# Norm work from GpSimd to VectorE, float32 products inside the norms, and a gate in three groups

## The chip, the cores and the metric

The kernel runs on one core of a Trainium2 chip. The metric is the device time of one execution in microseconds (us). A core has a matrix engine (TensorE, PE in the profile), a vector engine (VectorE, DVE), a scalar engine (ScalarE, ACT), a general one (GpSimd, POOL) and an engine that here only issues transfers (SyncE, SP). Each engine works through its own row of instructions in order and waits on the others by semaphores.

## The reference

Two blocks follow one another on 512 tokens of width 1024, with two layers each. A layer of the first block has four parts, each behind a residual and a LayerNorm; the second block has RMS norms, attention and a memory of 256 tokens.

```python
def first_block(x, p, ...):
    for i in range(DEPTH):                      # DEPTH = 2, ALPHA = sqrt(2)
        x = layer_norm(ALPHA * x + 0.5 * swiglu(x, ffn_w_in[i, 0], ffn_w_out[i, 0]), ...)
        mix = token_mix(x, mix_w_in[i], ...)
        x = layer_norm(ALPHA * x + mix, ...)
        x = layer_norm(ALPHA * x + 0.5 * swiglu(x, ffn_w_in[i, 1], ffn_w_out[i, 1]), ...)
        ple = jax.nn.sigmoid(x @ ple_w_gate[i] + ple_b_gate[i]) * (p[i] @ ple_w_proj[i])
        x = layer_norm(ALPHA * x + ple, ...)
    return x

def second_block(x, mem, ...):
    for i in range(DEPTH):                      # layer A: dilated attention, layer B: axial
        h = rmsnorm(x, norm_g[i])
        mem_h = rmsnorm(mem, mem_norm_g[i])
        ...
        o_mem = memory_attention(q_mem, mem_h, w_mem_kv[i], ...)   # kv = mem_h @ w_kv
        y = jnp.concatenate([o_mix, o_mem], axis=-1) * jax.nn.silu(gate)
        x = x + jnp.einsum('bse,ed->bsd', y, w_out[i])
    return x
```

The embedding p[i] is 512 x 256, ple_w_proj[i] is 256 x 1024, ple_w_gate[i] 1024 x 1024, w_mem_kv[i] 1024 x 1024.

## The kernel before

Features lie on the 128 partitions: x is eight feature tiles (KD = 8) of 128 x 512 tokens. Most work on tokens goes in two halves of 256 (HALF), so that one half's norm can run under the other half's products.

**Split products.** A float32 product is made of three products in a reduced type (fp32r in the profile): both operands are split into a high part (a cast on ScalarE) and a low part (x minus the high part), and hi·hi, hi·lo and lo·hi are summed in PSUM. `weight` (L146) loads a weight, casts `whi` (L153) and subtracts `wlo` (L154), on VectorE or on GpSimd as the caller says; `mm3` (L190) and `mm3k` (L1151) issue the products.

**A LayerNorm** (class LN, L258) is fed by `add`, tile by tile: x is updated and its sum `ln_s` and square sum `ln_q` grow along the features (L296, L299 to L303). For the first tile a mean is estimated and subtracted from all eight (L283, L285). `begin` sums over the partitions by TensorE (`ln_st`, L315), makes mean and reciprocal root from them by some 17 tiny operations on 128x2 (L319 to L323 and `rsqrt` at L231 to L239), spreads both over the partitions by TensorE (`ln_M`, `ln_B`, L253) and subtracts the mean (L332). `end` multiplies by the root (L343), applies scale and bias on ScalarE (L345), and writes the split result `xh`, `xl` (L352, L353) for the next products.

**A layer of the first block** runs ffn(l, 0), mixer, ffn(l, 1) and ple (L1015), each with the norm of its end inside. An FFN's weights come as units; its last output tile is made half by half, and the first half's `begin` lies between the halves. `ple` first splits p and its projection matrix and makes the embedding (`ppp`, 96 fp32r products), then the gate (`pg`): feature tiles 0 to 3 at once, in four PSUM tiles (`mm3_side`), for both halves, then 4 to 7 for each half; a sigmoid (`sig`, L1055) and a product with the embedding end each tile and free its PSUM.

**Memory.** In layer 1's ple the memory tokens are normalized and split (`mem_parts`), and layer A's keys and values (`p_mkv`) are made in three pieces between the steps of the gate and its norms; the RMS norm of layer A follows (`from_time`, `scale_time`, `write_time`). Layer B's keys and values are made between layers A and B (L1773).

**Order.** The tile framework's scheduler orders each engine's row, the transfers on SP's queue too; in the mixer TensorE's order is woven by hand. What is ready when depends on the buffer pools: five slots each for high and low parts of weights, two for loaded weights, and four each for two kinds of PSUM tiles.

Of the kernel before, what the change touches and what calls it, by code (L numbers as in the profile page):

```python
# [33 lines left out]
class Kern:  # L34
# [124 lines left out]
    def unit(self, src, eng=None, spare=False):  # L159

        if not spare:
            hi, lo = self.weight(src, D, eng)
            return [tuple(a[:, k * 128:k * 128 + 128] for a in (hi, lo)) for k in range(KD)]
        nc = self.nc
        st = self.pst.tile([128, D], F, name="wst", tag="wst")
        nc.sync.dma_start(out=st, in_=src)
        out = []
        for at in (slice(0, 512), slice(512, 1024)):
            hi, lo = self.t2(dt=FR, name="gwh"), self.t2(dt=FR, name="gwl")
            nc.scalar.copy(hi, st[:, at])  # L170
            (eng or nc.vector).tensor_sub(lo, st[:, at], hi.bitcast(F))
            out += [tuple(a[:, k * 128:k * 128 + 128] for a in (hi, lo)) for k in range(4)]
        return out
# [841 lines left out]
def ple(K, l, x, xh, xl, ln, rms=None, aside=None):  # L1015

    nc = K.nc
    V, A, G = nc.vector, nc.scalar, nc.gpsimd
# [3 lines left out]
    ph, pl = [], []  # L1022
    for k in range(2):
        st = K.t2(name="p_st")
        nc.sync.dma_start(out=st, in_=K.i["p"][l, :, k])
        ph.append(K.t2(dt=FR, name="p_h"))
        pl.append(K.t2(dt=FR, name="p_l"))
        K.split(ph[k], pl[k], st)
    Wp = []
    for j in range(2):  # L1030
        a, b = K.weight(K.i["ple_w_proj"][l, :, j * D:j * D + D], D)
        Wp.append((a.rearrange("p (f k c) -> p f k c", f=4, k=2), b.rearrange("p (f k c) -> p f k c", f=4, k=2)))

    pp = []
    for f in range(KD):
        p = K.acc(name="ppp")
        K.mm3(p, [((Wp[f // 4][0][:, f % 4, k], Wp[f // 4][1][:, f % 4, k]), (ph[k], pl[k])) for k in range(2)])
        c = K.t2(name="pp")
        A.copy(c, p)
        pp.append(c)  # L1040

    def unit(f, spare=False):
        return K.unit(K.i["ple_w_gate"][l, f], None if spare else nc.gpsimd, spare)

    def some(fs, W, tk):

        ps = {f: K.acc((128, 256), name="pg") for f in fs}
        parts = [(xh[:, k, tk], xl[:, k, tk]) for k in range(KD)]
        if fs[0] == 0:
            K.mm3_side([(ps[f], W[f], parts) for f in fs])  # L1050
# [871 lines left out]
```

## Time and profile before

| | us |
|---|---|
| median of 3 runs (lowest to highest) | 3540.33 (3538.97 to 3543.59) |
| the profiled execution, its own time | 3544.78 |
| its span in the trace | 3543.0 |
| TensorE busy | 3410.4 |
| VectorE busy | 1946.4 |
| ScalarE busy | 1245.0 |
| GpSimd busy | 723.7 |

Busy is the time in which an instruction of the engine was under way in the trace; the span is the time from the profile's first event to its last, and 1.8 us of the execution lie outside of it. The profile is of one execution, and its time is 4.5 us above the median of the runs.

### The profile page before, as it was taken

What the parts mean: (1) busy time and instruction counts of PE and PEld (TensorE: products, weight loads), DVE (VectorE), ACT (ScalarE), POOL (GpSimd) and SP (SyncE); (2) the same over time, 40 slices, a digit from 0 to 9 for tenths busy, and PEclk for the clock granted to TensorE, in tenths of its full rate; (3) what the DMA queues carried; (4) which work ended last, traced back from release to release, by engine and by line L of the source; (5) the groups of instructions that cost most, each with busy time, mean ns of one, the idle gap of its engine ahead of it and who ended that gap; (6) DMA issues with size and microseconds to landing.
All of it is one profiled execution on the core that took longest, in us unless ns stands there. A gap on an engine that the chain in (4) does not pass through costs nothing. (4 is left out here: it accounts for less than half of the span.)

```text
span 3543.0 us, 46065 instructions
## 1 busy us (share of the span) xinstructions
PE 3410.4 (96%) x17964; PEld 2900.1 (82%) x17964; DVE 1946.4 (55%) x4167; ACT 1245.0 (35%) x2104; POOL 723.7 (20%) x560
## 2 busy tenths in 40 slices
PE   8999999999999799999999999987999999999998
PEld 7888987788887788888978888876888888887777
DVE  3333665563334733346665533367867767649665
ACT  3322435332223332224353322244333333334332
POOL 0002412450012500123135200234122212111100
PEclk9999999999999899999999999997999999999999
DMA  4323211123232132232011222333222222243112
GB/s 154 109 87 98 85 36 49 37 84 101 95 92 87 48 107 98 87 93 84 34 36 61 84 100 87 98 97 122 86 85 71 69 87 73 75 133 115 54 47 79
DMA packets 91657, 294.40 MB, mean 83 GB/s; under 512 B 14256, under 2 KB 16944, under 8 KB 91312
## 3 DMA queue, kind: packets, MB, share of 16 engines
q1 hardware_dynamic: 91440, 291.47, 25.4%
q8 instruction: 141, 2.31, 0.3%
q14 instruction: 76, 0.62, 0.1%
HBM read 283.96 MB, written 7.47 MB: 82 GB/s over the span
## 5 line engine op out<-in xcount | busy, mean ns | idle before, releaser
L154 DVE TENSOR_TENSOR wlo<-wst,whi 128x1024 fp32r<-128x1024 f32 (+1 forms) x403 | 479.4, 1190 | 726.5 <-ACT whi L153 722.5
L153 ACT CAST whi<-wst 128x1024 fp32r<-128x1024 f32 (+1 forms) x520 | 530.3, 1022 | 881.1 <-issue 305.3
L188 PE MATMUL pgu<-xh,wlo 128*128 128x512 f32 (+1 forms) x1504 | 569.0, 379 | 0.2 <-ACT silu L374 0.2
L188 PE MATMUL pgu<-xl,whi 128*128 128x512 f32 (+1 forms) x1504 | 564.7, 378 | 0.0
L154 POOL TENSOR_TENSOR wlo<-wst,whi 128x1024 fp32r<-128x1024 f32 x117 | 282.0, 2416 | 577.0 <-ACT whi L153 566.7
L188 PE MATMUL pgu<-xh,whi 128*128 128x512 f32 (+1 forms) x1504 | 385.4, 379 | 12.3 <-ACT xh L176 9.1
L188 PEld LDWEIGHTS pgu<-xh,whi 128*128 128x128 f32 x1504 | 287.3, 191 | 63.8 <-ACT xh L176 9.1
L188 PEld LDWEIGHTS pgu<-xh,wlo 128*128 128x128 f32 x1504 | 287.6, 191 | 51.8 <-ACT silu L374 0.6
L188 PEld LDWEIGHTS pgu<-xl,whi 128*128 128x128 f32 x1504 | 285.0, 191 | 51.9 <-DVE xl L177 0.8
L1157 PE MATMUL p_in<-whi,xl 128*128 128x512 f32 (+1 forms) x800 | 305.1, 383 | 5.8 <-DVE xl L1307 4.5
L1157 PE MATMUL p_in<-wlo,xh 128*128 128x512 f32 (+1 forms) x800 | 305.8, 383 | 0.0
L1157 PE MATMUL p_in<-whi,xh 128*128 128x512 f32 (+1 forms) x800 | 305.2, 382 | 0.0
L285 POOL TENSOR_TENSOR x<-x,ln_c 128x256 f32<-128x256 f32 (+1 forms) x84 | 95.9, 1174 | 970.5 <-ACT ln_c L282 970.5
L188 PE MATMUL pfo<-hl,whi 128*128 128x512 f32 (+1 forms) x792 | 282.7, 366 | 0.0
L188 PE MATMUL pfo<-hh,wlo 128*128 128x512 f32 (+1 forms) x792 | 282.3, 365 | 0.0
L375 DVE TENSOR_TENSOR silu<-silu,pgu 128x512 f32<-128x512 f32 (+1 forms) x94 | 61.4, 653 | 225.1 <-PE pgu L188 190.9
L188 PE MATMUL pmx<-xl,whi 128*128 128x512 f32 (+1 forms) x480 | 180.3, 379 | 0.0
L1157 PEld LDWEIGHTS p_in<-whi,xl 128*128 128x128 f32 x800 | 151.6, 189 | 33.9 <-DVE xl L1307 4.6
L188 PE MATMUL pmx<-xh,wlo 128*128 128x512 f32 (+1 forms) x480 | 178.7, 373 | 0.0
L1157 PEld LDWEIGHTS p_in<-wlo,xh 128*128 128x128 f32 x800 | 151.7, 190 | 27.7 <-issue 2.6
L1157 PEld LDWEIGHTS p_in<-whi,xh 128*128 128x128 f32 x800 | 151.5, 189 | 27.6 <-issue 2.4
L188 PEld LDWEIGHTS pfo<-hh,wlo 128*128 128x128 f32 x792 | 149.4, 189 | 24.2
(376 smaller groups left out, 6468.7 us busy)
## 6 DMA issues: line engine op xcount, KB each, us to landing
wst<-in_ffn_w_in SPq DMA_DIRECT2D x176, 512.0 KB, 3.4
wst<-in_ffn_w_out SPq DMA_DIRECT2D x64, 512.0 KB, 3.5
wst<-in_wa_qk SPq DMA_DIRECT2D x48, 512.0 KB, 3.3
wst<-in_ffn_w_out SPq DMA_DIRECT2D x32, 384.0 KB, 3.1
wst<-in_mix_w_qkv SPq DMA_DIRECT2D x24, 512.0 KB, 3.5
wst<-in_wa_v SPq DMA_DIRECT2D x24, 512.0 KB, 3.3
wst<-in_w_gate SPq DMA_DIRECT2D x24, 512.0 KB, 3.2
wst<-in_w_out SPq DMA_DIRECT2D x32, 384.0 KB, 3.1
```

The costliest lines, as they stand in the source:

```text
L153: nc.scalar.copy(hi, st)
L154: sub = (eng or nc.vector).tensor_sub(lo, st, hi.bitcast(F))
L188: return self.nc.tensor.matmul(out, lhsT=lhsT, rhs=rhs, start=start, stop=stop)
L285: nc.gpsimd.tensor_sub(self.y[:, k, tk], self.y[:, k, tk], c)
L375: nc.vector.tensor_mul(s, s, ps[1])
L1157: K.nc.tensor.matmul(out, lhsT=w, rhs=x, start=(j == 0), stop=(j == n - 1))
```

## The change

Four things are done together.

1. GpSimd's work in the norms and the weight splits goes to VectorE: the mean's subtractions (84), the square sums (60), the low parts `xl` (56, for which the cast `xh` goes from VectorE to ScalarE), and 116 of the 117 `wlo` of 128x1024, of which 16 vanish with the splits below.
2. The embedding is a class of its own, `Embed`. It loads p and the projection unsplit (three transfers of 512 KB, into slots of the split weights) and multiplies in plain float32, one call in place of three products. Its 16 calls for feature tiles 0 to 3 are issued after the FFN's last output tile, the other 16 after the second half's `begin`.
3. The gate has three groups: feature tiles 0 to 3 side by side for each half, tile 4 for both halves in one PSUM tile, and 5 to 7 for each half.
4. The memory's keys and values are plain float32 products too, for both layers, in layer 1's norms; the results wait in DRAM. Nothing of it is left between layers A and B.

```diff
+    def raw(self, pool, src, n):
+        t = pool.tile([128, n], F, name="wraw", tag="whi" if pool is self.pwh else "wlo")
+        self.nc.sync.dma_start(out=t, in_=src)
+        return t
...
-                nc.gpsimd.tensor_sub(self.y[:, k, tk], self.y[:, k, tk], c)
+                nc.vector.tensor_sub(self.y[:, k, tk], self.y[:, k, tk], c)
...
-        if f < KD - 2:
-            nc.gpsimd.tensor_add(q, q, sq)
-        elif f == KD - 2:
+        if f == KD - 2:
...
-                nc.vector.tensor_copy(xh[:, ks, tk], y)
-                nc.gpsimd.tensor_sub(xl[:, ks, tk], y, xh[:, ks, tk].bitcast(F))
-def ffn(K, l, j, x, xh, xl, ln, aside=None, load=None):
+                nc.scalar.copy(xh[:, ks, tk], y)
+                nc.vector.tensor_sub(xl[:, ks, tk], y, xh[:, ks, tk].bitcast(F))
...
-        wh, wl = K.weight(w_in[l, j, 2 * f + u], D, nc.gpsimd if (f < 4 if load is None else f == 0 and u) else None)
+        wh, wl = K.weight(w_in[l, j, 2 * f + u], D, nc.gpsimd if load and f == 0 and u else None)
...
     W = out_units(KD - 1)
+    if ahead:
+        ahead.load()
     out_tile(KD - 1, W, HALF[0])
     ln.begin(HALF[0])
     out_tile(KD - 1, W, HALF[1])
+    if ahead:
+        ahead.products(0, 4)
     ln.end(HALF[0], xh, xl)
     ln.begin(HALF[1])
+    if ahead:
+        ahead.products(4, KD)
     ln.end(HALF[1], xh, xl)
...
-        wh, wl = K.weight(src, D, nc.gpsimd)
+        wh, wl = K.weight(src, D)
...
+class Embed:
+    def __init__(self, K, l):
+        self.K, self.l, self.out = K, l, []
+    def load(self):
+        K, i = self.K, self.K.i
+        self.p = K.raw(K.pwh, i["p"][self.l].rearrange("p k s -> p (k s)"), D).rearrange("p (k s) -> p k s", k=2)
+        self.W = [K.raw(K.pwl, i["ple_w_proj"][self.l, :, j * D:j * D + D], D).rearrange("p (f k c) -> p f k c", f=4, k=2)
+                  for j in range(2)]
+    def products(self, f0, f1):
+        K = self.K
+        for f in range(f0, f1):
+            p = K.acc(name="ppp")
+            for k in range(2):
+                K.mm(p, lhsT=self.W[f // 4][:, f % 4, k], rhs=self.p[:, k], start=(k == 0), stop=(k == 1))
+            c = K.t2(name="pp")
+            K.nc.scalar.copy(c, p)
+            self.out.append(c)
...
+    def some(f, W, tk):
+        p = K.acc((128, tk.stop - tk.start), name="pg")
+        K.mm3(p, list(zip(W, [(xh[:, k, tk], xl[:, k, tk]) for k in range(KD)])))
+        add(f, p, tk)
...
+    first, last = range(4), range(5, KD)
+    W = [K.unit(K.i["ple_w_gate"][l, f]) for f in first]
+    for tk in HALF:
+        ps = [K.acc((128, 256), name="pg") for f in first]
+        K.mm3_side([(ps[f], W[f], [(xh[:, k, tk], xl[:, k, tk]) for k in range(KD)]) for f in first])
+        for f in first:
+            add(f, ps[f], tk)
+    some(4, K.unit(K.i["ple_w_gate"][l, 4]), ALL)
+    W = {f: K.unit(K.i["ple_w_gate"][l, f]) for f in last}
+    if rms:
+        aside(0)
+    for f in last:
+        some(f, W[f], HALF[0])
+    ln.begin(HALF[0])
+    for f in last:
+        some(f, W[f], HALF[1])
+    ln.end(HALF[0])
     ln.begin(HALF[1])
     rms.from_time(HALF[0])
     aside(1)
-    rms.scale_time(HALF[0], ln.lead[0])
+    rms.scale_time(HALF[0])
     rms.write_time(HALF[0])
     ln.end(HALF[1], lead=False)
     rms.from_time(HALF[1])
+    aside(2)
     rms.scale_time(HALF[1])
     rms.write_time(HALF[1])
-    aside(2)
+    aside(3)
...
+def mem_tokens(K, l, R):
     g = load_small(K, K.i["mem_norm_g"][l], (128, KD), "mng")
-    hh, hl = Pieces(tiles[:4]), Pieces(tiles[4:])
-    for j, h in enumerate(mem_load(K)):
+    t = mem_load(K)
+    for j, h in enumerate(t):
         for i in range(2):
             k = 2 * j + i
             K.nc.vector.scalar_tensor_tensor(h[:, i], h[:, i], g[:, k:k + 1], R, op0=OP.mult, op1=OP.mult)
-        K.split(hh.t[j], hl.t[j], h)
-    return hh, hl
-def mem_kv(K, l, hh, hl, mk, mv, eng=None, which=(0, 1)):
-    for s in which:
+    return t
+def mem_kv(K, l, s, h, out):
+    W = [K.raw((K.pwh, K.pwl)[u % 2], K.i["w_mem_kv"][l, s, u], D).rearrange("p (k c) -> p k c", k=2) for u in range(4)]
+    if s == 0:
+        kn = load_small(K, K.i["mem_kn_g"][l], (128, 128), "mkn")
+    for t in range(2):
+        p = K.acc((128, HM, 128), name="p_mkv")
+        for k in range(KD):
+            K.mm(p, lhsT=h[k // 2][:, k % 2, t * 128:t * 128 + 128], rhs=W[k // 2][:, k % 2], start=(k == 0),
+                 stop=(k == KD - 1))
         if s == 0:
-            kn = load_small(K, K.i["mem_kn_g"][l], (128, 128), "mkn")
-        W = chunk512(K, K.i["w_mem_kv"][l, s], eng)
-        for t in range(2):
-            tk = slice(t * 128, t * 128 + 128)
-            p = K.acc((128, HM, 128), name="p_mkv")
-            yield from mm3k(K, p, [((hh(k, tk), hl(k, tk)), (W[k // 2][0][:, k % 2], W[k // 2][1][:, k % 2]))
-                                   for k in range(KD)])
-            if s == 0:
-                norm_heads(K, p, HM, lambda h: kn, None, [m[:, :, tk] for m in mk])
-            else:
-                K.nc.scalar.copy(mv[t], p.rearrange("p h e -> p (h e)"))
+            norm_heads(K, p, HM, lambda h: kn, None, [m[:, :, t * 128:t * 128 + 128] for m in out])
+        else:
+            K.nc.scalar.copy(out[t], p.rearrange("p h e -> p (h e)"))
...
+                    for m, kv in MEM[stage - 1]:
+                        out = [K.t2(name="mem_kv") for _ in range(2)]
+                        mem_kv(K, m, kv, tokens[m], out if kv else [t.rearrange("p (h n) -> p h n", n=256) for t in out])
+                        for j in range(2):
+                            nc.sync.dma_start(out=memkv[m][:, kv * 1024 + j * 512:kv * 1024 + j * 512 + 512], in_=out[j])
...
-            drive(mem_kv(K, 1, *hold["parts"], mk, mv))
```

On TensorE the scheduler's order at the end of layer 0's second FFN was this before (`pfo` is the FFN's output, line numbers are each kernel's own):

```order
L188 MATMUL pfo<-hh,whi 128x256 x11
...
L315 MATMUL ln_st<-ones,ln_s 128x1 x2
L315 MATMUL ln_st<-ones,ln_q 128x1 x2
L315 MATMUL ln_st<-ones,x 128x1 x2
L315 MATMUL ln_st<-ones,ln_sq 128x1 x2
...
L188 MATMUL ppp<-p_h,wlo 128x512 x4
L188 MATMUL ppp<-p_l,whi 128x512 x4
```

and is this now:

```order
L183 MATMUL pfo<-hh,whi 128x256 x11
L183 MATMUL ppp<-wraw 128x512 x5
...
L183 MATMUL ppp<-wraw 128x512
L308 MATMUL ln_st<-ones,ln_s 128x1 x2
L308 MATMUL ln_st<-ones,ln_q 128x1 x2
L183 MATMUL ppp<-wraw 128x512 x2
L308 MATMUL ln_st<-ones,x 128x1 x2
L308 MATMUL ln_st<-ones,ln_sq 128x1 x2
L183 MATMUL ppp<-wraw 128x512 x6
...
L183 MATMUL ppp<-wraw 128x512 x2
L183 MATMUL pg<-xh,whi 128x256
```

The rows left out are the broadcasts ln_B and ln_M. The embedding's products moved from behind the norm into it, 16 calls in all, and the gate's first product follows them.

On VectorE the chain of the norm between the mixer and the second FFN of layer 0 (first half; `pmo` is the mixer's output) ended thus before:

```order
L239 SCALAR_TENSOR_TENSOR ln_r<-rs_b,rs_n 128x2
L249 CAST bc_h<-ln_r 128x2
L250 TENSOR_TENSOR bc_l<-ln_r,bc_h 128x2
L332 TENSOR_TENSOR x<-x,ln_M 128x2x256 x4
L271 SCALAR_TENSOR_TENSOR x<-pmo,x 128x256
L343 TENSOR_TENSOR x<-x,ln_B 128x2x256
```

and ends thus now:

```order
L234 SCALAR_TENSOR_TENSOR ln_r<-rs_b,rs_n 128x2
L244 CAST bc_h<-ln_r 128x2
L154 TENSOR_TENSOR wlo<-wst,whi 128x1024
L245 TENSOR_TENSOR bc_l<-ln_r,bc_h 128x2
L325 TENSOR_TENSOR x<-x,ln_M 128x2x256 x4
L294 SCALAR_TENSOR_TENSOR ln_q<-ln_q,ln_sq 128x256
L266 SCALAR_TENSOR_TENSOR x<-pmo,x 128x256
L336 TENSOR_TENSOR x<-x,ln_B 128x2x256 x2
L154 TENSOR_TENSOR wlo<-wst,whi 128x1024
```

Splits of the next FFN's weights, which were GpSimd's, stand in the chain; another stands eight rows ahead of the first of these rows.

On TensorE the end of layer 1's gate was followed by memory products alone before (`gwh` and `gwl` are parts of the gate's weights, `mem_p` of the memory tokens):

```order
L188 MATMUL pg<-xl,gwh 128x256
L188 MATMUL pg<-xh,gwh 128x256 x8
L1157 MATMUL p_mkv<-whi,mem_p 128x512
L1157 MATMUL p_mkv<-wlo,mem_p 128x512
L1157 MATMUL p_mkv<-whi,mem_p 128x512 x2
```

and now the sums of the first half's norm stand between them:

```order
L183 MATMUL pg<-xl,whi 128x256
L183 MATMUL pg<-xh,whi 128x256 x8
L183 MATMUL p_mkv<-wraw,mem_t 128x512 x8
L308 MATMUL ln_st<-ones,ln_s 128x1 x2
L183 MATMUL p_mkv<-wraw,mem_t 128x512 x4
L308 MATMUL ln_st<-ones,ln_q 128x1 x2
L183 MATMUL p_mkv<-wraw,mem_t 128x512 x10
...
L183 MATMUL p_mkv<-wraw,mem_t 128x512 x2
```

All 64 calls of both layers' memory now lie in this stretch, in pieces of 2 to 12 between the norms' sums, broadcasts and transposes.

## Rows read from the trace of the kernel before

**Rows 1.** Page, part 1: busy time, share of the span and instructions of each engine.
```profile
PE 3410.4 (96%) x17964; PEld 2900.1 (82%) x17964; DVE 1946.4 (55%) x4167; ACT 1245.0 (35%) x2104; POOL 723.7 (20%) x560
```

**Rows 2.** Busy time by stretch (start:end us), all engines; columns in its first line.
```profile
core 0: us, PE busy (x) PEld busy (x) DVE busy (x) ACT busy (x) POOL busy (x), PEclk, DMA share, GB/s
1115.50:1142.70 27.20, 18.83 (x78) 15.06 (x76) 21.89 (x42) 15.41 (x29) 18.49 (x12) 0.69 0.24 78
1142.70:1203.96 61.26, 51.48 (x395) 50.37 (x393) 40.81 (x47) 21.10 (x42) 39.84 (x32) 0.94 0.22 70
1203.96:1243.40 39.44, 30.99 (x226) 30.62 (x226) 29.44 (x69) 13.99 (x27) 14.55 (x11) 0.83 0.09 28
2323.94:2473.80 149.86, 113.11 (x679) 103.18 (x678) 115.14 (x246) 74.68 (x148) 72.36 (x54) 0.83 0.32 107
735.40:775.60 40.20, 33.55 (x234) 33.12 (x235) 29.30 (x56) 13.15 (x27) 16.30 (x11) 0.83 0.12 40
375.39:420.02 44.63, 41.42 (x317) 40.66 (x317) 33.84 (x76) 20.66 (x50) 22.21 (x13) 0.92 0.23 71
3181.12:3204.68 23.56, 23.09 (x106) 18.76 (x105) 20.43 (x45) 13.18 (x21) 2.07 (x2) 1.00 0.57 201
3204.68:3231.00 26.32, 24.97 (x118) 20.54 (x118) 24.23 (x85) 11.76 (x25) 2.46 (x4) 1.00 0.29 101
```

**Rows 3.** Idle time of PE by what ended it: us in total, times, longest.
```profile
PE ln_B L253 <- DVE bc_l L250: 16.8, 6, 5.1
PE pg L188 <- ACT sig L1055: 16.7, 6, 4.8
PE rms_B L253 <- DVE bc_l L250: 7.5, 1, 7.5
```

**Rows 4.** Timeline of DVE, norm before layer 0's second FFN: start, us, engine, line, operation.
```profile
728.78 0.16 DVE L319 TENSOR_SCALAR ln_m<-ln_st 128x2 f32<-128x2 f32 x1 [0.74 <-PE ln_st L315]
...
732.13 2.38 DVE L235 TENSOR_TENSOR rs_a<-rs_n 128x2 f32<-128x2 f32 x1
...
736.62 2.24 DVE L250 TENSOR_TENSOR bc_l<-ln_r,bc_h 128x2 fp32r<-128x2 f32 x1
```

**Rows 5.** Timeline of POOL, the same stretch.
```profile
732.09 2.41 POOL L154 TENSOR_TENSOR wlo<-wst,whi 128x1024 fp32r<-128x1024 f32 x1 [0.67 <-ACT whi L153]
```

**Rows 6.** Timeline of DVE, the norm after layer 0's second FFN, its first half.
```profile
1110.57 0.16 DVE L319 TENSOR_SCALAR ln_m<-ln_st 128x2 f32<-128x2 f32 x1 [2.88 <-PE ln_st L315]
...
1113.32 0.16 DVE L250 TENSOR_TENSOR bc_l<-ln_r,bc_h 128x2 fp32r<-128x2 f32 x1
```

**Rows 7.** Timeline of PE, the same norm.
```profile
1117.58 0.88 PE L315 MATMUL ln_st<-ones,ln_sq 128*128 128x1 f32 x4
...
1129.58 2.08 PE L188 MATMUL ppp<-p_l,whi 128*128 128x512 f32 x4 [4.33 <-DVE p_l L177]
```

**Rows 8.** Timeline of PE in layer B's attention: plain float32 products.
```profile
3422.63 1.02 PE L1646 MATMUL att_p<-kT,qT 128*128 128x512 f32 x2
3423.49 0.81 PE L1404 MATMUL att_o<-att_t,vB 128*128 128x256 f32 x3
```

**Rows 9.** Groups by line and shape on PE: xcount, busy us, mean ns of one record.
```profile
L1646 PE MATMUL att_p<-kT,qT 128*128 128x512 f32 x64 | 31.7, 593 | 0.0
```

**Rows 10.** The same columns as in 2, instructions of tile p_mkv alone.
```profile
3187.26:3203.74 16.48, 16.48 (x71) 13.21 (x71) 0.62 (x3) 0.59 (x1) 1.00 0.51 175
```

**Rows 11.** Costliest groups by line on POOL: xcount, busy us, mean ns, idle before.
```profile
L154 POOL TENSOR_TENSOR wlo<-wst,whi 128x1024 fp32r<-128x1024 f32 x117 | 282.0, 2416 | 577.0 <-ACT whi L153 566.7 <-DVE xl L177 9.9
```

**Rows 12.** Groups by line and shape on DVE.
```profile
L154 DVE TENSOR_TENSOR wlo<-wst,whi 128x1024 fp32r<-128x1024 f32 x339 | 417.8, 1233 | 492.6 <-ACT whi L153 488.8 <-PE p_in L1157 0.9 <-PE att_T L183 0.9
L303 DVE TENSOR_TENSOR ln_q<-ln_q,ln_sq 128x256 f32<-128x256 f32 x8 | 3.4, 425 | 0.5
```

**Rows 13.** Busy time of line 154 (DVE, POOL) and of all engines inside layer 0's mixer.
```profile
400.00:680.00 280.00, 0.00 (x0) 60.42 (x25) 1.00 0.15 46
460.00:480.00 20.00, 14.87 (x97) 13.08 (x96) 19.79 (x43) 6.39 (x15) 5.53 (x2) 1.00 0.23 79
```

More of the change, by code (lines that the diff above doesn't have):

```diff
@@ L157, in weight, with unit @@
         return hi, lo
[L159 to L173, printed above, removed]
+    def unit(self, src):
+        hi, lo = self.weight(src, D)
+        return [tuple(a[:, k * 128:k * 128 + 128] for a in (hi, lo)) for k in range(KD)]
+    def raw(self, pool, src, n):
+        t = pool.tile([128, n], F, name="wraw", tag="whi" if pool is self.pwh else "wlo")
+        self.nc.sync.dma_start(out=t, in_=src)
+        return t
     def split(self, hi, lo, x):
@@ L1021, in ple @@
     K.table(SIGMOID)
[L1022 to L1050, printed above, removed]
-        for f in fs:
-            if fs[0]:
-                K.mm3(ps[f], list(zip(W[f], parts)))
-            s = K.t2((128, 256), name="sig")
-            K.looked.append(A.activation(s, ps[f], AF.Sigmoid, bias=bg[:, f:f + 1]))
-            V.tensor_mul(s, s, pp[f][:, tk])
-            ln.add(f, s, tk, 1.0 / ALPHA)
@@ L1059, in ple, with add @@
-    first, second = (0, 1, 2, 3), (4, 5, 6, 7)
-    W = {f: unit(f) for f in first}
-    if not rms:
-        for tk in HALF:
-            some(first, W, tk)
-        W = {f: unit(f) for f in second}
-        some(second, W, HALF[0])
-        ln.begin(HALF[0])
-        some(second, W, HALF[1])
+    def add(f, ps, tk):
+        s = K.t2((128, tk.stop - tk.start), name="sig")
+        K.looked.append(A.activation(s, ps, AF.Sigmoid, bias=bg[:, f:f + 1]))
+        V.tensor_mul(s, s, pp[f][:, tk])
+        ln.add(f, s, tk, 1.0 / ALPHA)
@@ L1072, in ple @@
         return
-    W.update((f, unit(f, True)) for f in second)
-    some(first, W, HALF[0])
-    aside(0)
-    some(second, W, HALF[0])
-    ln.begin(HALF[0])
-    some(first, W, HALF[1])
-    ln.end(HALF[0], lead=False)
-    some(second, W, HALF[1])
     K.table(EXP)
+    ln.end(HALF[0])
     ln.begin(HALF[1])
@@ L1102 @@
 SCALE = 128 ** -0.5
+MEM = ((0, 0), (0, 1)), ((1, 0), (1, 1)), ()
 NEG = -1.0e30
@@ L1473, in evac @@
                    [qm.pair(e)[:, :, c * 128:c * 128 + 128] for e in (0, 2)])
-    yield from project(K, xh, xl, chunk512(K, K.i["w_qm"][l], None if l else K.nc.gpsimd), 512, evac)
+    yield from project(K, xh, xl, chunk512(K, K.i["w_qm"][l]), 512, evac)
 def gates(K, l, es, xh, xl, O, Y):
@@ L1707, in program @@
         xd = aside.tile([128, KD, S], F, name="xd")
-        memd = aside.tile([128, 2304], F, name="memd")
+        memd = aside.tile([128, 256], F, name="memd")
+        memkv = [aside.tile([128, 2048], F, name="memkv") for l in range(DEPTH)]
         eps = LN_EPS / ALPHA ** 2
@@ L1724, in program @@
                     x = mixer(K, l, xh, xl, LN(K, None, *load_ln(K, l, 1), eps))
-                    ffn(K, l, 1, x, xh, xl, LN(K, x, *load_ln(K, l, 2), eps))
+                    embed = Embed(K, l)
+                    ffn(K, l, 1, x, xh, xl, LN(K, x, *load_ln(K, l, 2), eps), ahead=embed)
                     if l < DEPTH - 1:
-                        ple(K, l, x, xh, xl, LN(K, x, *load_ln(K, l, 3), eps))
+                        ple(K, l, x, xh, xl, embed.out, LN(K, x, *load_ln(K, l, 3), eps))
                 g = load_small(K, ins["norm_g"][0], (128, KD), "rmsg")
-                parts = []
-                mk = [K.t2((128, 2, 256), name="mem_k") for _ in range(2)]
-                mv = [K.t2(name="mem_v") for _ in range(2)]
+                tokens = []
                 def memory(stage):
@@ L1765, in reload_a @@
                 hold["x"] = slab()
-                hold["parts"] = mem_parts(K, 1, R, [K.tv((128, 2, 256), name="mem_p", dt=FR) for _ in range(6)] +
-                                          [K.tn((128, 2, 256), name="mem_p", dt=FR) for _ in range(2)])
+                nc.sync.dma_start(out=mem_all, in_=memkv[1])
             rms = RMS(K, lambda f: hold["x"](f), xh, xl, g)
```

29 lines of the change are left out of this document (12 added, 17 removed).

## The prediction

> **What bounds the kernel now.** The page's first part comes first: TensorE is busy 96% of the span, VectorE 55%, GpSimd 20% [rows 1]. So the kernel is a row of products, and a change can win only where TensorE has gaps or does work that it needn't. The windows say where: in the three stretches of layer 0 from its second FFN's last product to the next FFN's first, TensorE is busy 18.8 of 27.2 us, 51.5 of 61.3 and 31.0 of 39.4, at granted clocks of 0.69, 0.94 and 0.83 of full, so that part of each ran at the lower level (1.2 GHz) [rows 2]. The last gate of layer 1 and the norms behind it (2323.9 to 2473.8) are busy 113.1 of 149.9. The list of TensorE's waits names the releasers: the norm's broadcasts wait on VectorE (ln_B 16.8 us in 6 times, rms_B 7.5 in one), the gate's products on the sigmoids that free PSUM (16.7 in 6) [rows 3].
>
> Why VectorE is late there is read from three timelines. In the norm before layer 0's second FFN its chain of tiny operations on 128x2 lasts from 728.78 to 736.62 + 2.24 = 738.86: 10.1 us, with single ones of 2.38 and 2.24 us [rows 4]. While the 2.38 us one stands (732.13 to 734.51), GpSimd subtracts a weight's low part, 732.09 to 734.50 [rows 5]. The same chain without such a neighbour, 1110.57 to 1113.48, lasts 2.9 us, each operation 0.16 [rows 6]. So a GpSimd operation on two tensors holds up VectorE's operation on two tensors for as long as it lasts: 2.4 us for a split which VectorE itself does in 1.23 [rows 11, 12].
>
> **The change, part by part.** The sum is made against the profiled execution (3544.8 us), 4.5 above the runs' median of 3540.3; the same difference is then taken from the median. A measurement of this kernel tells about 0.2%, 7 us, from no change.
>
> **Embedding, layer 0.** Before, 96 products follow the FFN, after a wait of 4.33 us for p's low part [rows 7]; the stretch takes 27.2 us and the gate begins at its end. Now 32 plain float32 calls stand in the norm, 16 of them after the FFN's last product by the order of TensorE. The price of such a call of 128x512: line 1646 issues 32 (8 heads by 4 tiles) which leave 64 records, so a call is a pair [rows 9]; a pair is 3422.63 to 3423.49, 0.86 us [rows 8]. 16 calls are 13.8 us; the norm's sums and broadcasts, at about 0.2 us each (four sums 0.88, [rows 7]), are 3.1: 16.9 us against 27.2, **-10.3**. The half-clock share of that stretch goes with its idle time, since TensorE now has work throughout. Cover: half 0's normalized tile is ready about 15 us in, just before the products end, and the gate's first splits (4 of 1.23 us on VectorE, for which the raw tiles leave slots free late) fit in the same time. If they don't fit, up to 4 us come back; without the sums' waits it is 1 us better: -11 to -6.
>
> The Trainium skill ("FP8 and Floating Point Precision", TensorE Precision Notes) says that true FP32 takes four passes through the array. Four of this kernel's fp32r products would be 0.93 us, so by it the 96 float32 calls cost 6.7 us more than by the row, which gives 3.7 products; the row is used.
>
> **Gate, layer 0.** 192 products of 128x512 size at 16.48 / 71 = 0.232 us [rows 10] are 44.6 us; the stretch takes 61.3, with 9.8 idle and about 3.7 (6% of it) given to the lower clock [rows 2]. The order now leaves one turn-over of four PSUM tiles at once instead of three, then feature tile 4 at full width, then three. I let one wait of about 5 us stay and some 5 of starts and small sums: 54.8, **-6.5** (0 if each of the sigmoid waits, at most 4.8, stays; -10 if none does). Behind it half 0's sums now stand after all gate products, so half 0's chain is exposed where half of it was covered: its 2.9 to 10.1 us, less what was exposed already, **+1** (0 to +4) on 39.4.
>
> **Layer 1's gate, norms and memory** (149.9 us). TensorE's work there is now 16 embedding and 64 memory calls at 0.86 = 68.8, the gate 44.6, and sums, broadcasts and transposes about 16: 129.4. Uncovered remain the gate's waits (6.5), the norm of the last half ahead of the first projection (7.5, as the one rms_B wait is now [rows 3]), and one chain that the in-order memory products don't fill, about 6.5; with 2.6 of lower clock that is 152.5, **+2.6**. Ends: -10 if the memory calls fill two of the three waits too (13 us), +13 if they stand ahead of a chain's sums twice (two chains of about 5). This stretch pays for both layers' memory products.
>
> **Between layers A and B.** Layer 1's 96 fp32r memory products leave; they filled 23.1 of 23.6 us after layer A's output [rows 2], 96 x 0.232 = 22.3. They are the cover of layer B's norm, which then shows: a chain of 2.9, its broadcasts and eight scalings, casts and subtractions of about 0.4 to 0.7 each in a pipeline, some 13 us until the second half can be projected, and about 3.3 of lower clock as in the other norms. -22.3 + 16.3 = **-6** (-12 to -1).
>
> **Norms before the second FFNs** (40.2 us, two of them). GpSimd's three splits leave the chain, but by the order three of 1.23 us now stand in VectorE's row among its operations. 10.1 becomes 2.9 + 3.7 + the tile work that stands between, about 7.4: **-2.7 each, -5.4**. Ends: -6 each if the splits fall into waits; 0 if each operation behind them waits in full. **Norms before the mixers** (44.6 us, two): a split now stands ahead of the last tile's addition and the cast goes to ScalarE: +1.5 each, **+3** (0 to +6). The sums in the middle of an FFN (84 subtractions and 60 additions at 0.43 us [rows 12]) lie under its products; if VectorE had no room there, 62 us would show.
>
> **Mixers.** In 280 us of layer 0's, 25 splits keep GpSimd busy 60.4 us [rows 13]. Moved, they are 25 x 1.23 = 31 us of VectorE's time, in a unit that has stretches at 19.8 busy of 20 [rows 13]; in return up to 60 us of hold-ups end. Between +31 and -29 on VectorE, of which TensorE sees only the full stretches: I take **-1 each, -2** (-10 to +10).
>
> **Sum**: -10.3 - 6.5 + 1 + 2.6 - 6 - 5.4 + 3 - 2 = -23.6: the profiled execution would be 3521.2, the median 3516.7, say **3517**.
>
> **Rivals.**
> *VectorE becomes the bound.* 100 moved splits are 123 us on an in-order engine; a split that stands ahead of a tiny operation delays TensorE by 1.23. Place: the mixers' full stretches and the norms' chains. The terms above take some 10 us of it. If 24 us more of the 123 show, the gain is gone; at a third in all (41 us) it is 3540 - 24 + 31 = 3547. For it: 19.8 of 20 busy, and the order. Against: hold-ups of 2.4 us end for 1.23 of work, so that VectorE's sum hardly grows. Chance 0.13. The Trainium skill ("Perfetto Trace Analysis", Optimizing Scalar/DVE Operations) speaks both ways: where VectorE is saturated, offloading to GpSimd may make sense, but the two share a port, so it might not help; [rows 4, 5] agree with the second half.
> *Only the embedding gains*; the gate's waits stay and the rest nets to nothing: 3540 - 10 = 3530. For it: each term behind has an end near zero. Chance 0.2.
> *Memory products in TensorE's row hold up layer 1's norms*: +13 for +2.6 there, 3527. For it: they are issued ahead of sums in the order. Chance 0.15.
> *The hold-ups cost more than I count*: all waits on ln_B and rms_B end, and half the mixers' idle time: another 24 us less, 3493. Against it: splits stand in the same chains now. Chance 0.12.
> My forecast: 0.4.
>
> **Range.** 8 in 10 lie between the last rival (3494) and no change (3540); the likeliest case has 3506 to 3528 by its terms' ends, taken together but not all at once. VectorE's rival is half no change, half slower, and some of the others' tails reach it: faster 0.81, same 0.1, slower 0.09.
>
> **What would show it.** After the second FFNs' last product the first gate product stands about 17 us later, with 16 pairs of 0.86 between; VectorE's 128x2 operations all at 0.16; one rest of about 5 us in the gate; p_in of layer B some 22 us nearer to the last p_out but with an idle stretch between its halves. It is wrong if TensorE's idle time in the mixers grows, if the chains stay at 10 us with splits in them, or if the float32 products run above 0.86.

## The result, and the profile after

The median of four runs is 3487.23 us (3482.38 to 3491.48), the kernel before 3539.65 in the same series: a ratio of 0.9849, interval 0.9832 to 0.9866, so 53 us less. Forecast were 24, with 3494 as the lower end: the sign was right, the size was not. The profiled execution took 3484.36 us, 60.4 less than that of before. The page's first part after, the line that answers to [rows 1]:

```profile
PE 3389.2 (97%) x17820; PEld 2848.5 (82%) x17820; DVE 1931.5 (55%) x4389; ACT 1246.2 (36%) x2120; POOL 199.3 (6%) x238
```

GpSimd lost 524 us of work, and VectorE, which took it over, is busy 15 us less than before. TensorE's idle time fell from 3543.0 - 3410.4 = 132.6 us to 3482.6 - 3389.2 = 93.4, and its busy time by another 21.2. TensorE's waits after, which answer to [rows 3]:

```profile
PE pg L183 <- ACT sig L1047: 8.1, 3, 3.4
PE rms_B L248 <- DVE bc_l L245: 3.3, 2, 2.0
PE ln_B L248 <- DVE bc_l L245: 2.6, 1, 2.6
```

The waits on the norm's broadcast fell from 16.8 us to 2.6, those on the gate's sigmoids from 16.7 to 8.1. The same stretches as in [rows 2], by windows (stretch, its length, then busy time of PE, PEld, DVE, ACT, POOL, the granted clock and the DMA's share): embedding, gate, what follows it, layer 1's ple in one piece, A to the end of layer B's first projections, and both mixers' output products.

```profile
1103.53:1119.39 15.86, 15.86 (x58) 8.44 (x56) 12.65 (x33) 11.24 (x22) 0.00 (x0) 1.00 0.32 100
1119.39:1171.57 52.18, 48.76 (x368) 47.11 (x366) 39.24 (x79) 25.48 (x48) 0.00 (x0) 0.97 0.22 72
1171.57:1187.03 15.46, 7.43 (x37) 7.16 (x37) 14.27 (x49) 8.31 (x16) 0.00 (x0) 0.64 0.19 68
2278.12:2428.08 149.96, 136.31 (x680) 94.90 (x678) 105.66 (x305) 67.25 (x141) 0.00 (x0) 0.96 0.38 135
679.48:730.79 51.31, 48.40 (x400) 47.79 (x400) 34.38 (x86) 15.92 (x28) 0.00 (x0) 1.00 0.22 73
1853.36:1904.67 51.31, 48.40 (x400) 47.79 (x400) 34.45 (x86) 15.91 (x28) 0.00 (x0) 1.00 0.21 73
```

For the last two, the mixers' output products, the prediction had no figure as stretches; of what is in them it priced the norm's chain alone. Before they were, by the same view:

```profile
681.00:742.80 61.80, 54.21 (x405) 53.32 (x404) 34.82 (x60) 16.74 (x30) 37.76 (x32) 0.89 0.22 76
1889.70:1951.60 61.90, 54.31 (x405) 53.41 (x403) 35.41 (x60) 17.13 (x30) 37.77 (x32) 0.88 0.23 76
```

The same products, 10.5 us less in each: 4.7 of them idle time (7.6 to 2.9), 5.8 busy time, since the granted clock rose from 0.89 to 1.00. Two waits make up the difference. The first stands in the first microseconds. Timelines of VectorE, GpSimd and TensorE of the kernel before, ahead of the first output products (idle time and its releaser in brackets):

```profile
682.75 2.38 DVE L177 TENSOR_TENSOR mxl<-sc_o,mxh 128x512 fp32r<-128x512 f32 x1 [0.68 <-ACT mxh L176]
...
682.23 2.34 POOL L154 TENSOR_TENSOR wlo<-wst,whi 128x1024 fp32r<-128x1024 f32 x1 [3.04 <-ACT whi L153]
...
685.17 0.58 PE L188 MATMUL pmo<-mxl,whi 128*128 128x256 f32 x1 [2.03 <-DVE mxl L177]
```

and of VectorE and TensorE after:

```profile
681.73 0.68 DVE L172 TENSOR_TENSOR mxl<-sc_o,mxh 128x512 fp32r<-128x512 f32 x1
...
682.47 0.39 PE L183 MATMUL pmo<-mxl,whi 128*128 128x256 f32 x1 [0.95 <-DVE mxl L172]
```

A split of 0.68 us stood 2.38 us beside GpSimd's. TensorE's two waits there are 3.06 us together before (one of 1.03 ahead of these) and 1.90 after, and the 10.2 us behind them read by windows, before and then after:

```profile
684.20:694.40 10.20, 8.22 (x36) 7.92 (x37) 2.07 (x4) 1.20 (x3) 3.52 (x6) 0.50 0.17 54
...
682.50:692.70 10.20, 9.19 (x74) 8.99 (x75) 5.29 (x15) 1.89 (x5) 0.00 (x0) 1.00 0.19 53
```

The granted clock is 0.50, the lower level (1.2 GHz), behind the longer wait, and TensorE gets through 36 products; at 1.00 it gets through 74.

The second wait is the norm's own: near the stretch's end TensorE waited for the chain of [rows 4], which lies in this stretch, and the clock was low behind it too. TensorE's wait and the stretch around it, before:

```profile
738.92 0.48 PE L253 MATMUL ln_B<-ident_r,bc_l 128*128 128x128 f32 x1 [3.52 <-DVE bc_l L250]
...
735.00:742.80 7.80, 4.28 (x24) 4.08 (x23) 7.66 (x16) 2.35 (x5) 3.06 (x2) 0.78 0.40 135
```

After, this broadcast does not wait: the chain ends at 730.37 and the broadcast starts at 730.63. It also stands behind the last output product now, where 14 of them stood behind it before, so that the order has a part in it. By these rows each wait is worth about half of the 10.5 us, an estimate: 1.2 us of idle time and 4.1 of busy time (half of the 8.22) at the first, 3.5 and 1.7 at the second.

### The profile page after: what moved, and what is told of

It is laid out like the page before. It is cut to its first block, busy times and chain, and to the rows that moved or that the text cites. A ratio compares the mean times of both kernels' runs of the same rounds, so it can differ in the third digit from the quotient of the medians.

```text
span 3482.6 us, 45462 instructions
## 1 busy us (share of the span) xinstructions
PE 3389.2 (97%) x17820; PEld 2848.5 (82%) x17820; DVE 1931.5 (55%) x4389; ACT 1246.2 (36%) x2120; POOL 199.3 (6%) x238
## 4 chain that ended last, share of the span: by engine, by line
PE 94%; DVE 4%; ACT 1%; issue 1%; DMA 1%; SPq 0%; ACTq 0%; DVEq 0%
PE pgu L183 28%; PE p_in L1159 15%; PE pfo L183 14%; PE pmx L183 8%; PE p_gate L1159 4%; PE p_out L1159 3%; PE pmo L183 2%; PE pg L183 2%; PE att_o L1405 2%; PE p_mkv L183 1%; PE att_T L178 1%; PE pU L183 1%; PE pZ L183 1%; PE nh_t L178 1%; DVE wlo L154 1%; PE pL L183 1%
## 5 line engine op out<-in xcount | busy, mean ns | idle before, releaser
L154 DVE TENSOR_TENSOR wlo<-wst,whi 128x1024 fp32r<-128x1024 f32 (+1 forms) x503 | 599.4, 1193 | 762.2 <-ACT whi L153 756.5
L153 ACT CAST whi<-wst 128x1024 fp32r<-128x1024 f32 (+1 forms) x504 | 513.9, 1021 | 911.1 <-issue 289.7
L368 DVE TENSOR_TENSOR silu<-silu,pgu 128x512 f32<-128x512 f32 (+1 forms) x94 | 61.3, 652 | 226.2 <-PE pgu L183 197.6
L183 PEld LDWEIGHTS pfo<-hl,whi 128*128 128x128 f32 x792 | 149.3, 189 | 24.2
L183 PE MATMUL pfo<-hh,whi 128*128 128x512 f32 (+1 forms) x792 | 167.4, 366 | 0.0
```

The lines of the kernel that those rows point to most:

```text
L153: nc.scalar.copy(hi, st)
L154: sub = (eng or nc.vector).tensor_sub(lo, st, hi.bitcast(F))
L183: return self.nc.tensor.matmul(out, lhsT=lhsT, rhs=rhs, start=start, stop=stop)
L368: nc.vector.tensor_mul(s, s, ps[1])
```

## The experiments

Twelve kernels ran; each ratio is to the kernel before on the same chip (the changed kernel has 0.9849, interval 0.9832 to 0.9866).

| run | median us | ratio | interval |
|---|---|---|---|
| engines alone (e4) | 3489.67 | 0.9851 | 0.9836 to 0.9865 |
| all but the engines (e3) | 3524.98 | 0.9949 | 0.9933 to 0.9966 |
| splits back on GpSimd (e1) | 3498.11 | 0.9873 | 0.9858 to 0.9888 |
| norm work back on GpSimd (e2) | 3502.62 | 0.9885 | 0.9870 to 0.9899 |
| GpSimd works for nothing (e11) | 3558.46 | 1.0053 | 1.0036 to 1.0069 |
| late last split (e6) | 3492.79 | 0.9859 | 0.9845 to 0.9874 |
| memory as before (e7) | 3486.86 | 0.9846 | 0.9831 to 0.9861 |
| layer 1's memory between (e8) | 3479.92 | 0.9825 | 0.9808 to 0.9841 |
| gate in two groups (e9) | 3483.18 | 0.9833 | 0.9819 to 0.9848 |
| e8 and e9, tokens kept (e10) | 3475.05 | 0.9814 | 0.9799 to 0.9828 |
| half of layer 1's memory (e12) | 3491.16 | 0.9859 | 0.9844 to 0.9874 |
| e10, cast on VectorE (e13) | 3480.20 | 0.9818 | 0.9802 to 0.9835 |

The stages of six profiles in us, worked out from TensorE's records in each trace, from the end of one tile's last product to the next one's (or, for "to", to its first):

| stage | before | after | e4 | e3 | e11 | e10 |
|---|---|---|---|---|---|---|
| layer 0: norm and mixer to its output | 305.6 | 304.1 | 303.4 | 307.7 | 312.3 | 303.8 |
| mixer's output products | 61.8 | 51.3 | 51.3 | 59.8 | 63.5 | 51.3 |
| second FFN's last product to the gate | 27.2 | 15.9 | 27.4 | 16.0 | 15.9 | 15.9 |
| gate | 61.3 | 52.2 | 52.9 | 65.1 | 63.4 | 54.9 |
| gate's end to the end of layer 1's first FFN input | 257.2 | 257.8 | 255.3 | 257.1 | 264.6 | 254.0 |
| layer 1: norm and mixer | 306.4 | 301.8 | 302.0 | 306.7 | 312.0 | 303.5 |
| mixer's output products | 61.9 | 51.3 | 51.3 | 62.0 | 62.8 | 51.3 |
| FFN to the gate | 27.0 | 15.9 | 23.4 | 16.1 | 15.9 | 15.9 |
| gate | 63.3 | 53.5 | 62.7 | 55.3 | 55.4 | 52.1 |
| to layer A's projections | 59.5 | 80.6 | 49.2 | 79.9 | 80.7 | 62.3 |
| layer A | 707.5 | 704.0 | 710.6 | 705.3 | 705.4 | 704.3 |
| memory, layer B's projections | 192.4 | 183.1 | 192.6 | 180.0 | 184.5 | 195.7 |

From before to after these stages change by 59.8 of the spans' 60.4 us.

**The two halves of the change.** e3 is the changed kernel with GpSimd's work given back (two of its lines):

```diff
-                nc.vector.tensor_sub(self.y[:, k, tk], self.y[:, k, tk], c)
+                nc.gpsimd.tensor_sub(self.y[:, k, tk], self.y[:, k, tk], c)
...
-        wh, wl = K.weight(src, D)
+        wh, wl = K.weight(src, D, nc.gpsimd)
```

> The changed kernel with both the splits and the norm's work back on GpSimd: the embedding, the gate's groups and the memory of the change alone. By the stages of the two profiles these are worth about 34 us and the engines about 26. H: 3506 to 3516, with lower-clock stretches near those of the kernel before. O: 3487 to 3495.

e4 is the kernel before with those lines the other way round and nothing else:

> The kernel before with nothing but the engines changed: splits and the norm's work on VectorE, the normalized tile's cast on ScalarE. H: 3505 to 3518, with the output stretches of both mixers at 52 us for 62. O: 3530 to 3540. If it is above 3540, VectorE is the bound after all and the gain needs the other parts.

Neither range of theory H held: e3 came 9 us above its upper end, e4 15 below its lower one, so the engines are worth more than the stages of two profiles had let me think. The engines alone give 53 us, as much as the whole change; the rest alone gives 18. The two together don't add up to 71: on top of the engines the rest gives nothing that the ratios can tell (0.9849 against 0.9851). The first part of e4's page, then its output stretches and two more, by windows:

```profile
PE 3386.4 (97%) x17964; PEld 2878.8 (82%) x17964; DVE 1961.7 (56%) x4433; ACT 1273.0 (36%) x2160; POOL 199.6 (6%) x238
...
677.99:729.29 51.30, 48.39 (x401) 47.78 (x400) 34.39 (x86) 15.92 (x28) 0.00 (x0) 1.00 0.24 73
1861.56:1912.86 51.30, 48.38 (x400) 47.78 (x400) 34.40 (x86) 15.91 (x28) 0.00 (x0) 1.00 0.22 73
1129.26:1182.15 52.89, 49.33 (x395) 48.72 (x393) 37.33 (x81) 23.51 (x47) 0.00 (x0) 0.97 0.25 80
2285.86:2421.16 135.30, 111.50 (x679) 102.04 (x678) 109.95 (x291) 74.72 (x151) 0.00 (x0) 0.84 0.31 101
```

TensorE has as many products as before, 17964. Its idle time fell by 26.4 us (to 3492.6 - 3386.4 = 106.2) and its busy time by 24.0, with the granted clock's mean at 0.983 for 0.975: about half of the engines' gain is idle time, half busy time. VectorE is busy only 15 us more than before with all of GpSimd's 524 us. The third of the windows is layer 0's gate in its old two groups: 52.9 us, 61.3 before. So the gate's gain too is the engines'. The fourth is layer 1's ple with the old memory: 135.3, where the changed kernel takes 150.0.

The gate's longest wait before can be followed back, engine by engine:

```profile
1158.73 2.34 POOL L154 TENSOR_TENSOR wlo<-wst,whi 128x1024 fp32r<-128x1024 f32 x1 [11.82 <-ACT whi L153]
1158.96 2.39 DVE L283 TENSOR_TENSOR x<-x,ln_c 128x256 f32<-128x256 f32 x1 [3.81 <-ACT ln_c L282]
1161.39 0.42 ACT L287 ACTIVATE ln_q<-x 128x256 f32<-128x256 f32 x1 [2.46 <-DVE x L283]
1161.71 0.46 ACT L1055 ACTIVATE sig<-pg,bg 128x256 f32<-128x256 f32 x1
1162.22 0.58 PE L188 MATMUL pg<-xh,whi 128*128 128x256 f32 x1 [4.85 <-ACT sig L1055]
```

VectorE's subtraction of the mean, 0.43 us long in e4, stood 2.39 beside a split on GpSimd; ScalarE's square waited for it, the sigmoid that frees the PSUM tile stood behind the square, and TensorE waited 4.85 us. In e4 the longest such wait in this gate is 1.81.

Another reading would be that GpSimd's results were late. Before, TensorE's waits that GpSimd ended come to 0.9 us in all, those of VectorE and ScalarE to 14.6; so lateness can have made little of the 53.

**Splits or the norm's own work.** One of the two pairs of lines above is given back at a time.

> The changed kernel with the weight splits back on GpSimd (100 of 128x1024), the norm's own work still on VectorE. Theory H (GpSimd's operations hold up VectorE, TensorE waits longer for it, and behind such waits its clock falls): the mixers' output stretches, 51.5 us now, go back to about 60 each and the granted clock's lower level returns there; 3503 to 3518 us. Rival O (the new order and the embedding in the norm gave nearly all, the engine hardly matters): 3487 to 3493.

> The changed kernel with the norm's own work back on GpSimd (the mean's subtractions, the square sums, the low parts of the normalized tiles, with their casts back on VectorE), the weight splits on VectorE. H: fewer and shorter hold-ups than in the run with the splits, so 3490 to 3503. O: 3487 to 3491. A third possibility: the normalized tile's low part on VectorE is itself late, then faster than 3484.

In ratios the splits cost 0.0024 (8.5 us), the norm's work 0.0036 (13), both 0.0100 (35): more than the sum, by little more than the intervals allow. e2 is as theory H has it; e1 lies between its two ranges. The output stretches are 54.0 and 55.8 us with the splits back (60 were expected; the granted clock is 1.00 in the first), 51.3 and 51.3 with the norm's work back, 59.8 and 62.0 with both. The norm's work alone costs elsewhere: 2.0 and 4.9 us in the two norms and mixers, 3.2 behind layer 0's gate, 3.8 in layer A.

**The hold-up itself.** e11 leaves each engine's order as changed, and lets GpSimd subtract into a tile that nothing reads (one slot fewer in the common pool makes room for it):

```diff
+        if n == D and aside:
+            for q in range(2):
+                nc.gpsimd.tensor_sub(self.idle, self.idle, hi[:, q * 512:q * 512 + 512].bitcast(F))
...
-            with K.region(g=49):
+            with K.region(g=48):
```

> The changed kernel, every engine's order unchanged, but at each weight split of the mixers, the second FFNs' first eight units and the gates GpSimd subtracts two halves of the high part from a tile that nobody reads (2 x 128x512, work for nothing, with two operands from SBUF). Hold-up theory: VectorE is held up as in the kernel before and has the splits besides, so the time goes up by at least what giving the splits back to GpSimd cost (11 us): 3498 to 3520 us, with lower-clock stretches back. Rival (GpSimd's splits were merely late, since one takes 2.4 us, and an unread result holds up nobody): 3484 to 3490.

71 us above the changed kernel, and 38 above the upper end of what was expected. Its page, its GpSimd group, and VectorE's and GpSimd's timelines at the first mixer's end:

```profile
PE 3410.7 (96%) x17820; PEld 2867.0 (81%) x17820; DVE 2066.8 (58%) x4390; ACT 1246.1 (35%) x2120; POOL 563.2 (16%) x454
...
L158 POOL TENSOR_TENSOR idle<-idle,whi 128x512 f32<-128x512 f32 x216 | 364.3, 1686 | 1927.0 <-ACT whi L155 1916.5
...
689.00 1.70 DVE L159 TENSOR_TENSOR wlo<-wst,whi 128x1024 fp32r<-128x1024 f32 x1
690.63 1.75 DVE L177 TENSOR_TENSOR mxl<-sc_o,mxh 128x512 fp32r<-128x512 f32 x1
...
688.36 3.47 POOL L158 TENSOR_TENSOR idle<-idle,whi 128x512 f32<-128x512 f32 x2 [1.67 <-ACT whi L155]
```

VectorE is busy 135 us more for one instruction more, and in the traces the instructions of TensorE, VectorE and ScalarE stand in the same order as in the changed kernel: 364 us of unread work took 135 from VectorE. The split `mxl` (0.68 us) ends at 692.38, 0.55 after GpSimd's second operation: it stood until that was over. The hold-up goes both ways: GpSimd's operation takes 1.26 us at its shortest and 1.69 in the mean. That one engine's work lengthens the other's is thus shown, since no result passes between them. The 71 us are not all the hold-up's, though: ScalarE waited 16.2 us, in six times, until GpSimd had read a high part and its slot could be written again.

**Wait or clock.** e6 makes only the last split of each mixer late:

```diff
+        for _ in range(3 * i):
+            V.tensor_scalar(o, o, 1.0, None, op0=OP.mult)
         new_mixed(6 + i)
```

> The changed kernel with three multiplications by one (of 128x512, about 0.45 us each) ahead of the last split of each mixer, so that TensorE's wait at the start of the output products grows from 1.9 us to about 3.4, as long as in the kernel before. Clock theory: the lower level of TensorE's clock returns behind the longer wait for some 10 us, so each mixer loses 1.5 + 5 us: output stretches near 58 us for 51.3, 3497 to 3503 us in all. Rival, the wait alone counts: 3 us more in all, 3490, no lower clock there.

TensorE's two waits there, before the products on `mxh` and `mxl`, and the stretches:

```profile
682.06 0.39 PE L183 MATMUL pmo<-mxh,wlo 128*128 128x256 f32 x1 [3.13 <-ACT mxh L171]
682.79 0.58 PE L183 MATMUL pmo<-mxl,whi 128*128 128x256 f32 x1 [0.34 <-DVE mxl L172]
...
678.22:732.59 54.37, 49.89 (x400) 49.27 (x400) 35.64 (x89) 16.02 (x28) 0.00 (x0) 0.97 0.23 69
1855.24:1909.38 54.14, 49.66 (x401) 48.96 (x400) 35.68 (x89) 16.03 (x28) 0.00 (x0) 0.97 0.23 69
```

The waits grew by 1.57 us, the stretch by 3.1 and 2.8; the busy time grew by 1.5 and 1.3 for the same products. By windows the granted clock behind the wait is:

```profile
682.60:686.00 3.40, 3.21 (x15) 3.21 (x16) 0.14 (x1) 0.00 (x0) 0.00 (x0) 0.53 0.24 96
686.00:692.80 6.80, 5.79 (x47) 5.58 (x47) 4.59 (x13) 1.61 (x4) 0.00 (x0) 0.99 0.01 2
```

So the lower level did come, in both mixers, but for 3.4 us instead of ten, and cost 1.5 us where five were expected: the mechanism is there, at a third of the size. In time the run is not told apart from the changed kernel.

**The memory's place.** e7 puts its products back as they were, e8 puts layer 1's back between the layers but in float32 (lines of e8):

```diff
-MEM = ((0, 0), (0, 1)), ((1, 0), (1, 1)), ()
+MEM = ((0, 0),), ((0, 1),), ()
...
+            for s in range(2):
+                mem_kv(K, 1, s, hold["tok"], (mk, mv)[s])
```

> The changed kernel with the memory's products as before (three fp32r products each, layer 1's between layers A and B), their splits on VectorE; embedding, gate and engines as changed. If the memory's move into layer 1's norms is what cancels the other gains: the stretch from the gate to layer A's projection falls from 80.6 to about 50, the one between A and B grows by about 10, 3462 to 3474 us. Rival (that stretch is long since sums and chains stand behind each other there, whatever fills it): 3480 to 3490.

> The changed kernel with layer 1's memory back between layers A and B, but in plain float32 for both. 32 calls of 0.86 each way: the norm's stretch loses up to 27.5 us of the 80.6, the one between A and B gains about 27.5 less the 10.5 of waits and 6.8 of lower clock that it fills. Move is the cause: 3470 to 3480, some 10 above the run with fp32r (2 x 5.2 us by the prices of a call). Float32 is the cause instead: no better than 3484.

e7 falls as to its number: the stretch to layer A's projections shrank to 57.4 us, but its gate grew to 63.2 (a wait of 6.4 us in it), layer A to 709.5 and the part behind it to 193.0. e8 takes 61.1 for 80.6 and loses 5.5 in layer A and 12.6 behind it: a net of 1.4 us. Its time is in the range expected and its ratio 0.0024 better, but the intervals overlap. So neither run by itself shows that the move cost anything.

**The gate's groups.** e9 has `last = range(4, KD)` for layer 0, and tile 4 no longer alone.

> The changed kernel with layer 0's gate in two groups again (feature tiles 0 to 3, then 4 to 7 for each half). If the three groups give the 6.5 us of the prediction: 3492 to 3496. If the engines gave it, and the groups only expose the first half's norm: 3480 to 3488, with the stretch behind the gate shorter by 3.

Gate and what follows up to the end of the next FFN's input take 54.9 + 254.0 = 308.9 us; three groups 52.2 + 257.8 = 310.0. The three groups move some 3 us from the gate to behind it.

**A better version.** e10 joins e8 and e9 and keeps the scaled tokens in DRAM; e12 and e13 vary it.

```diff
+                        for j in range(4):
+                            nc.sync.dma_start(out=memtok[:, j * 512:j * 512 + 512], in_=tokens[1][j].rearrange("p k s -> p (k s)"))
```

> The version with layer 1's memory products between layers A and B in float32, with layer 0's gate in two groups, and with layer 1's scaled memory tokens kept in DRAM from layer 1's ple, so that VectorE scales nothing ahead of layer A's output. If the 5.5 us that layer A lost in the run before (709.5 for 704.0) are that scaling: 704 to 706 there, and 3468 to 3477 in all. If they are another wait: 709 and 3478 to 3482.

> As the version with kept tokens, but layer 1's keys in the norms of layer 1's ple and only its values between layers A and B, 16 calls of 0.86 us each. If the norms have room for 16 calls more than layer 0's 32 (their idle time is 15 us and lower clock costs some 13): 5 us faster than that version. If every call there costs its 0.86 us: 14 us come in there and 10 to 13 go between A and B, 1 to 4 us slower.

> The version with kept tokens and two gate groups, with one more part of the change undone: the cast xh of the normalized tile is VectorE's again. If ScalarE's cast is what makes the first product behind the mixers' norms start 1.7 us later than before (5.9 for 4.2 us after the last output product): 3468 to 3473, with 4.5 us there. If it is the splits in VectorE's row: no faster, 3474 to 3480, since the cast adds 0.68 us four times to that row.

e10 has 704.3 us in layer A, as said, and 3475 in all; its interval lies below that of the changed kernel. In the three stages that the memory touches it is 5.3 us below the changed kernel (18.3 fewer, 0.3 and 12.6 more). Its ple of layer 1, and the part from A on, where TensorE has no idle time left:

```profile
2276.58:2406.83 130.25, 111.06 (x607) 86.15 (x606) 97.38 (x271) 61.96 (x130) 0.00 (x0) 0.88 0.34 118
3111.15:3306.84 195.69, 195.69 (x833) 146.43 (x833) 148.05 (x464) 74.06 (x140) 27.18 (x42) 1.00 0.24 79
```

e12 fits neither expectation, 16 us above e10: 7.9 us more ahead of layer A, 6.9 fewer behind it, and 13 more in layer A itself (717.3), where TensorE waits 7.8 us in one piece for the first heads' norm on VectorE. e13 gains nothing: the first FFN product stands 6.6 us behind the mixer's last, 5.9 in e10, so giving the cast back to VectorE doesn't bring it earlier. Its second mixer has the same two waits as the changed kernel's, 1.90 us together, and yet the granted clock is 0.57 from 1856.00 to 1864.00 and the output stretch 53.8 us for 51.3.

## Why the prediction was wrong

**The step that failed** is the engines' part: "Norms before the second FFNs ... -2.7 each, -5.4", "norms before the mixers ... +3" and "mixers ... -1 each, -2". These three came to -4.4 us; by the stages they are 2 x -10.5 for the output products and -1.5 and -4.6 for the norms and mixers, -27. That is 23 of the 37 us between the forecast -23.6 and the -60.4 of the two profiles, and the engines alone are worth 53 over the whole program.

Why so small a figure: the chain's own length was costed, and rightly. After the change VectorE's timeline has it from 723.14 to 730.37, 7.2 us for 7.4 forecast, with the splits in it:

```profile
723.14 0.15 DVE L312 TENSOR_SCALAR ln_m<-ln_st 128x2 f32<-128x2 f32 x1
...
725.77 1.23 DVE L154 TENSOR_TENSOR wlo<-wst,whi 128x1024 fp32r<-128x1024 f32 x1
...
729.08 1.23 DVE L154 TENSOR_TENSOR wlo<-wst,whi 128x1024 fp32r<-128x1024 f32 x1
730.22 0.15 DVE L245 TENSOR_TENSOR bc_l<-ln_r,bc_h 128x2 fp32r<-128x2 f32 x1
```

What it is worth to TensorE was not: the 2.7 us are VectorE's, where TensorE lost a wait of 3.5 and, by the estimate above, 1.7 of busy time behind it. And the hold-up was priced in this chain alone, not at each other place where TensorE waits for VectorE. Two were missed. At a mixer's end one split held up for 1.7 us (2.38 for 0.68) made a wait that the lower clock followed. In the gate one subtraction held up for 2.0 us (2.39 for 0.43) stands at the head of a wait of 4.85; the gate took 61.3 us with GpSimd at work and 52.9 without, in the old groups. The clock was left out of every such term: 5.8 of the 10.5 us in an output stretch are busy time, and 24.0 of e4's 50.4.

The +1.5 for each norm before a mixer is right at the place itself: the mixer's first product stands 5.9 us behind the FFN's last, 4.3 before. The mixers behind that gained 3.1 and 6.1 us by the stages, where 1 each was forecast.

**Embedding**: right. -11.3 for -10.3, 15.9 us for 16.9, and 16.0 in e3 without the engines. The price of a call was right too. TensorE's timeline has twelve records, six calls, in one piece:

```profile
1112.39 5.40 PE L183 MATMUL ppp<-wraw 128*128 128x512 f32 x12
1117.22 0.62 PE L248 MATMUL ln_M<-ident_r,bc_l 128*128 128x128 f32 x1
```

The records follow one another by 0.43 us (the first by 0.51), so that the twelfth starts at 1117.19 and a call takes 0.86, as forecast. The missing microsecond is in the norm's sums and broadcasts, 2.1 us for 3.1. By the Trainium skill's four passes ("FP8 and Floating Point Precision", TensorE Precision Notes) a call would have been 0.93, an estimate with the prediction's 0.232 for a pass; the measured 0.86 is 3.7 such products, and decides.

**Gate**: -9.1 for -6.5, but the reason was wrong. Three groups are worth about nothing (e9), the engines 8.4 (e4); with GpSimd at work three groups took 65.1 (e3), 4 more than two.

**Behind the gate** +0.6 for +1: right. One reading there is off: the window of 39.4 us does not end at the next FFN's first product, which starts at 1216.35, but 27 us later; the sum does not rest on it. **Layer 1's ple** 149.96 for 152.5: right as a sum, by errors that cancel. TensorE is busy 136.3 us where 129.4 and 2.6 for the clock were forecast, and idle 13.7 for 20.5. The engines took 14.6 us from that stretch by themselves (135.3 in e4), and the memory ate it. **A to B** -9.3 for -6, inside its ends: right. **Layer A** had no term; it takes 3.5 us less.

**The rivals.** That VectorE becomes the bound is refuted: it is busy less than before with 222 instructions more, and 15 us more where the engines alone change (e4). The page "Perfetto Trace Analysis" of the Trainium skill (Optimizing Scalar/DVE Operations) had both halves of it; the half on the shared port is the one that holds here. The last rival, hold-ups that cost more than counted, was the right one in its mechanism: the waits on ln_B fell by 14.2 us, those on rms_B by 4.2. It had 0.12 and 3493, and left out the clock and the gate; 3487 lies below the range. "Only the embedding gains" is refuted by e4. That memory products hold up layer 1's norms is right in part at most: with layer 1's back between A and B and the tokens kept (e10) the three stages are 5.3 us shorter.

**What stays open.** Why equal waits had unequal clock losses: 3.06 us of waits at the first mixer's end were followed by 10.2 us at the lower level before, but by 3.4 in e3 (686.3 to 689.7); 1.90 us were followed by none in the changed kernel and by 6.8 in e13's second mixer. What a wait costs in clock is therefore read from a profile here, and not forecast. And how much the rest of the change gives over e4: its stages are -11.5 and -7.6 for the embedding, -9.2 for layer 1's gate, +31.4 in the stretch to layer A's projections and -16 behind it, about -13. The two profiled executions differ by 10.0, but e4's is 4.7 us above its median and the changed kernel's 2.9 below; the ratios differ by 0.0002 with intervals of 0.0015 (5 us) each way.

## What to carry to other kernels

Work that is off the critical path on GpSimd can still be on it: where its operations on two tensors lie beside VectorE's, count each at up to its whole length at every place that waits for VectorE, not in the chain alone that one is looking at. A wait of a few microseconds on TensorE is to be priced with the busy time behind it, read from the granted clock of that stretch; half of what the engines gave here (e4) was busy time. And parts that fill the same idle time don't add up: measure each alone and all but each before keeping them.
